# Encoder layer on one core: a feed forward's first weights loaded and split ahead of the last operands, and six pairs of the samples' features instead of four in the filling stream

## The chip, the cores and the metric

The kernel runs on one core of a Trainium2 chip. The metric is the device time of one execution in microseconds, the median of several runs. The core has a matrix engine (TensorE, PE; its weight loads are listed apart as PEld), a vector engine (VectorE, DVE), an activation engine (ScalarE, ACT), a general engine (GpSimd, POOL) and a queue that issues all of this kernel's transfers (SyncE, SP). Each of them works through its own list of instructions in a fixed order and waits at an instruction until what that instruction needs is there.

## What is computed

One layer of an encoder in float32: a gated linear recurrence and a sliding-window attention side by side, a cross-attention into 256 memory tokens, and a SwiGLU feed forward, each followed by a layer norm. It is applied to 1024 prompt tokens and to 8 sample sequences of 16 tokens, so 1152 rows of 1024 columns. The change lies in the feed forward:

```python
def swiglu(x, w_in, w_out):
    g, u = jnp.split(x @ w_in, 2, axis=-1)
    return (jax.nn.silu(g) * u) @ w_out

# post_blocks, last line
x = layer_norm(ALPHA * x + swiglu(x, w_ffn_in, w_ffn_out), ln_g[2], ln_b[2])
```

D_MODEL is 1024, and D_FF is 2816, that is 22 blocks of 128 features, worked in 11 pairs.

## The kernel before

The 1152 rows are nine tiles of 128: eight of the prompt and one (SAMPLE) that holds all the samples. A product in full precision is made of three matmuls: an operand is split into a rounded part ("hi", fp32r, made by a copy on ACT) and a remainder ("lo", made by a subtraction on DVE), and hi*hi, hi*lo and lo*hi are added up. `split` does this; `parts_of` does it for a tile of weights and puts the parts into w_hi and w_lo, of which there are four each.

**The feed forward's first half.** The eight prompt tiles are taken as a 2 x 2 block matrix (two halves of the rows by two halves of the 1024 columns), and each pair's weights too (a11, a12, a21, a22, 512 KB each). Strassen's scheme in Winograd's form needs seven products of 24 matmuls instead of eight: with a11, s1 = a21 + a22, s2 = s1 - a11, s4 = a12 - s2, s3 = a11 - a21, a12 and a22, against the operands B11, T1, T2, B22, T3, B21 and T4. POOL makes the sums s and T. `operands(ops, j, rows)` makes one quarter of the columns of all seven operands, from two token tiles: 16 transposes on PE, four copies on ACT into "stage", four subtractions on POOL into "tt", seven hi parts on ACT and seven lo parts on DVE (that of T4 on POOL). `all_operands` runs it for j = 0 to 3. `hidden(ops, i, then)` computes pair i of the features: it loads the four tiles of weights on SP (line 1003), forms the s, and runs the seven products in the order a11, s1, s2, s4, s3, a12, a22. A product's weights are split as it is issued.

**The samples.** Their features use plain float32 matmuls against the weights as loaded, 64 PE instructions in the trace a pair. In pairs 0 to FILL - 1 `filler` does it: it loads each of the four weight tiles a second time, into one of three w_raw tiles (line 971), 16 PE instructions a tile, which is called a chunk here. Each pair takes two of the four banks "a" of PSUM, and ends with three steps of `sample_gated`, one on ACT (line 959) and two on DVE (lines 960 and 961), and a store of the result (hs_scratch, line 962). Since there are four banks, pair i + 2 needs those of pair i, which the three steps read. In the later pairs `sample_pair` does it inside `hidden`, between the first and the second product, from the weights that are there already; in the last pair at the end.

**What sets the order.** The program is written by streams (generators) that an Order object takes in turn, by ranks and by a count of estimated matmul time. all_operands has rank 6 and filler rank 10, so the chunks stand between the operands of j and j + 1. The feed forward waits for both streams (`yield ready`, `yield filled`) and then goes through the eleven pairs. Within this the framework's scheduler may move an instruction a little on its engine. So all engines' lists are fixed when the program is built, SP's list of transfers too: a transfer that waits holds all that stand behind it.

Of the kernel before, what the change touches and what calls it, by code (L numbers as in the profile page):

```python
# [10 lines left out]
F32R = mybir.dt.float32r  # L11
# [7 lines left out]
P = 128  # L19
# [11 lines left out]
TILES = (0, 1, 3, 4, 5, 6, 7, 8)  # L31
SAMPLE = 2
PAIRS = FT // 2
FILL = 4
PARTS = ((0, 2), (2, 4), (4, 6), (6, 8), (8, 11))


# [65 lines left out]
def trunk(ctx, tc, I, O):  # L103
    nc = tc.nc
# [10 lines left out]
    wp = left.enter_context(tc.tile_pool(name="wp", bufs=1))  # L115
# [4 lines left out]
    N_SLOT, N_TA, N_RAW, N_W = 16, 8, 3, 4  # L120

    def bank(name):
        return pp[name][0].tile([P, 512], F32, name=name, tag=(pp[name] + (name,))[2], bufs=pp[name][1])
# [10 lines left out]
    def split(src, hi, lo, scale=None):  # L134
        if scale is None:
            S.copy(hi, src)  # L136
            V.tensor_tensor(lo, src, hi.bitcast(F32), op=ALU.subtract)  # L137
        else:
            S.activation(hi, src, AF.Copy, scale=scale)
            V.scalar_tensor_tensor(lo, src, scale, hi.bitcast(F32), op0=ALU.mult, op1=ALU.subtract)  # L140

    def raw_tile():
        return wp.tile([P, 1024], F32, name="w_raw", bufs=N_RAW)
# [8 lines left out]
    def mm3(out, a, b, start, stop, **kw):  # L152
        T.matmul(out, a[0], b[0], start=start, stop=False, **kw)
        T.matmul(out, a[0], b[1], start=False, stop=False, **kw)
        T.matmul(out, a[1], b[0], start=False, stop=stop, **kw)

    def cut(pair, *idx):
        return pair[0][idx], pair[1][idx]
# [3 lines left out]
    def cols(t, n=1):  # L162
        return slice(t * P, (t + n) * P)
# [17 lines left out]
    def transposes(src4, n=4):  # L181
        ps = bank("b")
        for j in range(n):
            T.transpose(ps[:, cols(j)], src4[:, cols(j)], ident)
        return ps
# [498 lines left out]
    def big(name, dt=F32):  # L684
        return p2.tile([P, 1024], dt, name=name, tag="big", bufs=10)
# [236 lines left out]
    def operands(ops, j, rows):  # L922

        b = {}
        for q in range(2):
            st = big("stage").rearrange("p (e k c) -> p e k c", e=2, k=4)
            for e in range(2):
                ps = transposes(rows[e][:, q * 512:q * 512 + 512])
                S.copy(st[:, e], ps.rearrange("p (k c) -> p k c", k=4))
                b[f"B{q + 1}{e + 1}"] = st[:, e]  # L930
        for n in range(4):
            if n % 2 == 0:
                tt = big("tt").rearrange("p (a k c) -> p a k c", a=2, k=4)
            b[f"T{n + 1}"] = tt[:, n % 2]
        for o, x, y in (("T1", "B12", "B11"), ("T2", "B22", "T1"), ("T3", "B22", "B12"), ("T4", "B21", "T2")):
            G.tensor_tensor(b[o], b[x], b[y], op=ALU.subtract)
        for o in OPS:
            hi, lo = (x[:, :, cols(j)] for x in ops[o])
            S.copy(hi, b[o])
            (G if o == "T4" else V).tensor_tensor(lo, b[o], hi.bitcast(F32), op=ALU.subtract)  # L940

    def all_operands(ops, rows, ready):
        got = list(rows)

        def load(j):
            got.insert(j, big("x2_row"))
            nc.sync.dma_start(out=got[j], in_=x2_dram[TILES[j]])

        for j in (0, 1, 2, 3, 4):
            load(j)  # L950
        yield 3500.0
        for j in range(4):
            operands(ops, j, (got[j], got[j + 4]))
            yield 6000.0
        order.set(ready, 1000.0)
# [8 lines left out]
    def filler(filled):  # L964

        for i in range(FILL):
            ps = [bank("a")[:, :256] for _ in range(2)]
# [14 lines left out]
    def sample_pair(i, ws):  # L982

        ps = bank("b")
        for e in range(2):
            for z in range(2):
                for kt in range(KT):
                    T.matmul(ps[:, cols(e * 2 + z)], ws[e][kt // 4][:, cols(z * 4 + kt % 4)], xs[:, kt],
                             start=kt == 0, stop=kt == KT - 1)
        g = ps.rearrange("p (e z t) -> p z e t", e=2, z=2)  # L990
        h = hs.rearrange("p (e t) -> p e t", e=2)
        sample_gated(i, h, [g[:, 0], g[:, 1]])

    def parts_of(src, hi, lo):
        split(src, hi, lo)
        return hi, lo

    def hidden(ops, i, then):

        def wt(name, j=None):  # L1000
            t = big(name)
            if j is not None:
                nc.sync.dma_start(out=t, in_=I["w_f1"][i, j])
            return t

        th = [raw_tile() for _ in range(2)]
        m1 = raw_tile()
        m1 = [m1[:, :512], m1[:, 512:]]
        a11, a21, a22, a12 = wt("a11", 0), wt("a21", 2), wt("a22", 3), wt("a12", 1)
        s1, s2, s4 = wt("s1"), wt("s2"), wt("s4")  # L1010
        G.tensor_tensor(s1, a21, a22, op=ALU.add)
        G.tensor_tensor(s2, s1, a11, op=ALU.subtract)
        G.tensor_tensor(s4, a12, s2, op=ALU.subtract)
        m0 = [big("m0") for _ in range(2)]

        t1, t2, t4 = m0[0][:, 512:], m0[1][:, 512:], m1[0]
        X, Z, W = [], [], []

        def product(bk, which, w, op, start):
            pair = parts_of(w, *(wp.tile([P, 1024], F32R, name=x, bufs=N_W) for x in ("w_hi", "w_lo")))  # L1020
            for z in range(2):
                if start:
                    bk.append(bank(which))
                for kt in range(4):
                    mm3(bk[z], cut(pair, ALL, cols(z * 4 + kt)), cut(ops[op], ALL, kt),
                        start and kt == 0, kt == 3, skip_group_check=not start)
                yield z

        def gated(t, gate, up):
            S.activation(t, gate, AF.Tanh, scale=0.5)  # L1030
            V.scalar_tensor_tensor(t, t, 1.0, gate, op0=ALU.add, op1=ALU.mult)
            V.scalar_tensor_tensor(t, t, 0.5, up, op0=ALU.mult, op1=ALU.mult)

        def store(o, src):

            nc.sync.dma_start(out=h_dram[:, OPS.index(o), :, i].rearrange("q p b c -> p q b c"),
                              in_=src.rearrange("p (q b c) -> p q b c", b=2, c=P))

        a, b = slice(0, 512), slice(512, 1024)
        for z in product(X, "a", a11, "B11", True):  # L1040
            S.copy(m0[z][:, a], X[z])
            yield
        last = i == PAIRS - 1
        if FILL <= i and not last:
            sample_pair(i, ((a11, a12), (a21, a22)))
        s3 = wt("s3") if last else a21
        G.tensor_tensor(s3, a11, a21, op=ALU.subtract)
        for z in product(Z, "b", s1, "T1", True):
            S.copy(m1[z], Z[z])
            yield  # L1050
        for z in product(X, "a", s2, "T2", False):
            S.copy(m0[z][:, b], X[z])
            yield
        for z in product(Z, "b", s4, "B22", False):
            V.tensor_tensor(m0[z][:, b], m0[z][:, b], Z[z], op=ALU.add)
            yield
        then()
        gated(th[0][:, b], m0[0][:, b], m0[1][:, b])
        for z in product(X, "a", s3, "T3", False):
            V.tensor_tensor(m1[z], m1[z], X[z], op=ALU.add)  # L1060
            yield
        gated(th[1][:, b], m1[0], m1[1])
        for z in product(W, "b", a12, "B21", True):
            V.tensor_tensor(m0[z][:, a], m0[z][:, a], W[z], op=ALU.add)
            yield
        gated(th[0][:, a], m0[0][:, a], m0[1][:, a])
        G.tensor_tensor(t1, th[0][:, b], th[0][:, a], op=ALU.subtract)
        G.tensor_tensor(t2, th[1][:, b], t1, op=ALU.subtract)
        G.tensor_tensor(th[0][:, b], th[1][:, b], th[0][:, b], op=ALU.subtract)
        for o, src in (("B11", th[0][:, a]), ("T1", t1), ("T2", t2), ("B22", th[1][:, b]), ("T3", th[0][:, b])):  # L1070
            store(o, src)
        for z in product(X, "a", a22, "T4", False):
            yield
        if last:
            sample_pair(i, ((a11, a12), (a21, a22)))
        gated(th[1][:, a], X[0], X[1])
        G.tensor_tensor(t4, th[1][:, a], t2, op=ALU.subtract)
        store("B21", th[1][:, a])
        store("T4", t4)
# [387 lines left out]
```

## Time and profile before

| what | value |
|---|---|
| time, median of 3 runs | 1707.23 us (1706.56 to 1713.33) |
| time of the profiled execution | 1704.64 us |
| span of its trace | 1702.9 us |
| samples' stream and operands, the first chunk at 845.6 to the last at 882.6 | 37 us |
| first product of pair 0 to the second product's start | 890.53 to 904.92 |
| eleven hidden pairs to their last matmul of samples | to 1382.2 |
| second half of the feed forward | from 1382.2 |

The times in the trace are microseconds from the span's start. L96 is the matmul's line, L100 the transposes', L136 and L137 the two halves of a split. The trace leaves out numbers in names, so a11, a12, a21 and a22 all read "a" where they are loaded, and s1, s2 and s4 read "s"; the bank "a" of PSUM has the same letter. "both" holds the samples' activations and their features. A bracket at a row's end is the time that the engine sat idle before it, and what ended it.

### The profile page before, as it was taken

Reading aid. Unit: us, or ns where it says so; the run is one execution under the profiler, and the core shown is the slowest. Engines: PE = TensorE matmul, PEld = TensorE weight load, DVE = VectorE, ACT = ScalarE, POOL = GpSimd, SP = SyncE. Lnnn points to the kernel's source line nnn. Section 1 sums busy time; section 2 is a strip of 40 time slices with the busy share of each in tenths; the row PEclk is TensorE's granted clock in tenths of the full one; section 3 lists DMA queues with packets and bytes.
Section 4 is the critical chain, followed back from the end, with each engine's and each line's share of the span. In section 5 each row is a group of like instructions: output and inputs, shape, how many; then the busy total and the mean of one; then the engine's idle time right before and its main releaser. Section 6 shows DMA issues by size and latency. Waiting matters only on the chain.

```text
span 1702.9 us, 24403 instructions
## 1 busy us (share of the span) xinstructions
PE 1620.7 (95%) x9065; PEld 1391.3 (82%) x9065; DVE 1134.6 (67%) x2021; ACT 674.4 (40%) x1365; POOL 495.7 (29%) x381
## 2 busy tenths in 40 slices
PE   8999999999999999999979999999999969988896
PEld 7998999999888987889877888888888857766674
DVE  6786788778488666786687454544444665767576
ACT  4543555446443544325263333323222333434321
POOL 1111111111000000000074443332333454676555
PEclk9999999999999999999998999999999988999998
DMA  7443343334974687556362333122222245333342
GB/s 239 143 160 122 102 148 104 98 118 137 314 274 154 197 278 268 198 171 236 115 205 78 104 115 117 66 74 86 95 92 96 93 164 180 105 118 118 103 146 95
DMA packets 114358, 247.91 MB, mean 146 GB/s; under 512 B 11840, under 2 KB 58048, under 8 KB 114240
## 3 DMA queue, kind: packets, MB, share of 16 engines
q1 hardware_dynamic: 114240, 246.36, 43.8%
q8 instruction: 71, 1.16, 0.3%
q14 instruction: 47, 0.39, 0.1%
HBM read 203.65 MB, written 42.60 MB: 145 GB/s over the span
## 4 chain that ended last, share of the span: by engine, by line
PE 77%; DVE 7%; DMA 6%; POOL 5%; ACT 2%; issue 2%; SPq 1%; POOLq 0%; ACTq 0%; DVEq 0%
PE a L96 48%; PE b L96 20%; PE x L96 3%; PE b L100 2%; DMA hq<-h_scratch 2%; PE z L96 1%; DVE w L1122 1%; PE s L96 1%; DMA raw<-in_w_f_dram 1%; PE w L96 1%; DVE y L1164 1%; DMA w_raw<-in_w_out_dram 1%; DMA w_raw<-in_w_fm_dram 1%; DMA w_raw<-in_w_f_dram 1%; DVE w_lo L137 1%
## 5 line engine op out<-in xcount | busy, mean ns | idle before, releaser
L137 DVE TENSOR_TENSOR w_lo<-w_raw,w_hi 128x1024 fp32r<-128x1024 f32 (+1 forms) x169 | 204.8, 1214 | 115.0 <-ACT w_hi L136 114.6
L136 ACT CAST w_hi<-w_raw 128x1024 fp32r<-128x1024 f32 (+1 forms) x169 | 174.6, 1034 | 206.1 <-PE a L96 77.4
L96 PE MATMUL a<-w_hi,q_hi 128*128 128x256 f32 (+1 forms) x576 | 197.4, 344 | 0.8 <-ACT kv_sb L270 0.7
L96 PE MATMUL a<-w_lo,q_hi 128*128 128x256 f32 (+1 forms) x576 | 196.9, 342 | 0.0
L96 PE MATMUL a<-w_hi,q_lo 128*128 128x256 f32 (+1 forms) x576 | 194.7, 338 | 0.0
L96 PE MATMUL a<-q_hi,w_hi 128*128 128x384 f32 x528 | 186.8, 354 | 7.3 <-ACT q_hi L136 4.3
L96 PE MATMUL a<-q_hi,w_lo 128*128 128x384 f32 x528 | 179.9, 341 | 0.0
L96 PE MATMUL a<-q_lo,w_hi 128*128 128x384 f32 x528 | 179.5, 340 | 0.0
L96 PE MATMUL x<-w,hh 128*128 128x512 f32 x344 | 115.0, 417 | 39.5 <-DVE y L1164 23.6
L137 DVE TENSOR_TENSOR w_lo<-a,w_hi 128x1024 fp32r<-128x1024 f32 x43 | 75.0, 1743 | 76.9 <-ACT w_hi L136 76.9
L96 PEld LDWEIGHTS a<-w_hi,q_hi 128*128 128x128 f32 x576 | 108.4, 188 | 15.6 <-ACT kv_sb L270 1.1
L96 PEld LDWEIGHTS a<-w_lo,q_hi 128*128 128x128 f32 x576 | 108.6, 189 | 13.3 <-issue 1.2
L96 PEld LDWEIGHTS a<-w_hi,q_lo 128*128 128x128 f32 x576 | 108.5, 188 | 12.7 <-issue 0.2
L96 PEld LDWEIGHTS x<-w,hh 128*128 128x128 f32 x344 | 66.6, 198 | 62.8 <-ACT hh L1152 15.7
L96 PEld LDWEIGHTS a<-q_hi,w_hi 128*128 128x128 f32 x528 | 100.5, 190 | 12.2 <-ACT q_hi L136 4.6
L699 POOL TENSOR_TENSOR rs<-rs,mhalf 128x1 f32<-128x1 f32 x18 | 17.2, 958 | 301.0 <-DVE rs L698 301.0
L96 PE MATMUL a<-T_h,w_hi 128*128 128x512 f32 x264 | 104.7, 396 | 0.0
L96 PE MATMUL a<-T_l,w_hi 128*128 128x512 f32 x264 | 104.7, 396 | 0.0
L96 PE MATMUL a<-T_h,w_lo 128*128 128x512 f32 x264 | 104.6, 396 | 0.0
L96 PEld LDWEIGHTS a<-q_lo,w_hi 128*128 128x128 f32 x528 | 100.7, 191 | 1.6 <-issue 0.9
L96 PEld LDWEIGHTS a<-q_hi,w_lo 128*128 128x128 f32 x528 | 100.2, 190 | 1.0 <-DVE w_lo L137 0.7
L1152 ACT CAST hh<-hq 128x512 fp32r<-128x512 f32 (+2 forms) x75 | 46.3, 619 | 133.2 <-DMA hq<-h_scratch 117.3
(308 smaller groups left out, 3930.4 us busy)
## 6 DMA issues: line engine op xcount, KB each, us to landing
a<-in_w_f_dram SPq DMA_DIRECT2D x44, 512.0 KB, 5.2
w_raw<-in_w_fm_dram SPq DMA_DIRECT2D x41, 512.0 KB, 3.9
h_scratch<-w_raw SPq DMA_DIRECT2D x55, 256.0 KB, 2.2
hq<-h_scratch SPq DMA_DIRECT2D x54, 256.0 KB, 2.7
w_raw<-in_w_tm_dram SPq DMA_DIRECT2D x24, 512.0 KB, 3.5
w_raw<-in_w_out_dram SPq DMA_DIRECT2D x24, 512.0 KB, 5.7
w_raw<-in_w_mq_dram SPq DMA_DIRECT2D x24, 512.0 KB, 4.2
w_raw<-in_w_mo_dram SPq DMA_DIRECT2D x24, 512.0 KB, 4.4
```

Of the source, the lines that this page charges most:

```text
L96: return self.eng.matmul(out, lhsT, rhs, **kw)
L100: return self.eng.transpose(out, in_, identity)
L136: S.copy(hi, src)
L137: V.tensor_tensor(lo, src, hi.bitcast(F32), op=ALU.subtract)
L699: G.tensor_tensor(rs, rs, mhalf[:, 0:1], op=ALU.pow)
L1122: (G if name in ("A21", "A22") else V).tensor_tensor(lo, src, hi.bitcast(F32), op=ALU.subtract)
L1152: S.copy(hi, q)
L1164: V.scalar_tensor_tensor(y[b, e][:, hs], y[b, e][:, hs], 1.0 if key in y else ALPHA, ps, op0=ALU.mult, op1=ALU.add)
```

## The change

`FILL` goes from 4 to 6, so `filler` computes the samples' features of pairs 4 and 5 too, with eight more loads and chunks, and `sample_pair` no longer runs in these two pairs. And pair 0's four weight tiles are loaded, and a11 split, by a new function `begin(0)`, which all_operands calls ahead of the operands of j = 3; `hidden` takes them from there, and calls begin itself in the other pairs.

```diff
--- before.py
+++ after.py
@@ -31,7 +31,7 @@
 TILES = (0, 1, 3, 4, 5, 6, 7, 8)
 SAMPLE = 2
 PAIRS = FT // 2
-FILL = 4
+FILL = 6
 PARTS = ((0, 2), (2, 4), (4, 6), (6, 8), (8, 11))
 
 
@@ -950,6 +950,8 @@
             load(j)
         yield 3500.0
         for j in range(4):
+            if j == 3:
+                begun.append(begin(0))
             operands(ops, j, (got[j], got[j + 4]))
             yield 6000.0
         order.set(ready, 1000.0)
@@ -995,19 +997,28 @@
         split(src, hi, lo)
         return hi, lo
 
+    begun = []
+
+    def begin(i):
+
+        def wt(name, j):
+            t = big(name)
+            nc.sync.dma_start(out=t, in_=I["w_f1"][i, j])
+            return t
+
+        a11, a21, a22, a12 = wt("a11", 0), wt("a21", 2), wt("a22", 3), wt("a12", 1)
+        return a11, a21, a22, a12, parts_of(a11, *both_parts())
+
+    def both_parts():
+        return tuple(wp.tile([P, 1024], F32R, name=x, bufs=N_W) for x in ("w_hi", "w_lo"))
+
     def hidden(ops, i, then):
 
-        def wt(name, j=None):
-            t = big(name)
-            if j is not None:
-                nc.sync.dma_start(out=t, in_=I["w_f1"][i, j])
-            return t
-
+        a11, a21, a22, a12, first = begun.pop() if begun else begin(i)
         th = [raw_tile() for _ in range(2)]
         m1 = raw_tile()
         m1 = [m1[:, :512], m1[:, 512:]]
-        a11, a21, a22, a12 = wt("a11", 0), wt("a21", 2), wt("a22", 3), wt("a12", 1)
-        s1, s2, s4 = wt("s1"), wt("s2"), wt("s4")
+        s1, s2, s4 = big("s1"), big("s2"), big("s4")
         G.tensor_tensor(s1, a21, a22, op=ALU.add)
         G.tensor_tensor(s2, s1, a11, op=ALU.subtract)
         G.tensor_tensor(s4, a12, s2, op=ALU.subtract)
@@ -1017,7 +1028,7 @@
         X, Z, W = [], [], []
 
         def product(bk, which, w, op, start):
-            pair = parts_of(w, *(wp.tile([P, 1024], F32R, name=x, bufs=N_W) for x in ("w_hi", "w_lo")))
+            pair = first if w is a11 else parts_of(w, *both_parts())
             for z in range(2):
                 if start:
                     bk.append(bank(which))
@@ -1043,7 +1054,7 @@
         last = i == PAIRS - 1
         if FILL <= i and not last:
             sample_pair(i, ((a11, a12), (a21, a22)))
-        s3 = wt("s3") if last else a21
+        s3 = big("s3") if last else a21
         G.tensor_tensor(s3, a11, a21, op=ALU.subtract)
         for z in product(Z, "b", s1, "T1", True):
             S.copy(m1[z], Z[z])
```

In the rows that follow, the lists of the built programs are shown, with the numbers of the tiles and the semaphores that each row waits for. The lines of the new program are counted anew (973 was 971, 964 was 962, 1006 was 1003, 962 and 963 were 960 and 961). First SP, from the load of the samples' pair 3, second chunk, on; before:

```order
L971 DMA w_raw_9793<-in_w_f1_dram 128x1024 [waits DMAHW4_49,DMAHW0_49,PE_49]
L971 DMA w_raw_9803<-in_w_f1_dram 128x1024 [waits DMAHW1_49,PE_49]
L971 DMA w_raw_9859<-in_w_f1_dram 128x1024 [waits DMAHW2_49,PE_49]
L962 DMA hs_scratch<-both_84 128x256 [waits DVE_49]
L1003 DMA a11_9876<-in_w_f1_dram 128x1024 [waits Activation_49,Pool_49]
L1003 DMA a21_9878<-in_w_f1_dram 128x1024 [waits Activation_49,Pool_49]
L1003 DMA a22_9880<-in_w_f1_dram 128x1024 [waits Pool_49]
L962 DMA hs_scratch<-both_84 128x256 [waits DMAHW3_49,DVE_49]
L1003 DMA a12_9882<-in_w_f1_dram 128x1024 [waits DMAHW4_49]
L1003 DMA a11_10133<-in_w_f1_dram 128x1024 [waits DMAHW5_49,Activation_49,Pool_49]
```

and with the change, at the same place:

```order
L973 DMA w_raw_9793<-in_w_f1_dram 128x1024 [waits DMAHW4_49,DMAHW0_49,PE_49]
L1006 DMA a11_9813<-in_w_f1_dram 128x1024 [waits Pool_49]
L973 DMA w_raw_9803<-in_w_f1_dram 128x1024 [waits DMAHW1_49,PE_49]
L1006 DMA a21_9815<-in_w_f1_dram 128x1024
L964 DMA hs_scratch<-both_84 128x256 [waits DVE_49]
L1006 DMA a22_9817<-in_w_f1_dram 128x1024
L1006 DMA a12_9819<-in_w_f1_dram 128x1024 [waits DMAHW2_49]
L973 DMA w_raw_9871<-in_w_f1_dram 128x1024 [waits DMAHW3_49,PE_49]
L973 DMA w_raw_9887<-in_w_f1_dram 128x1024 [waits DMAHW4_49,PE_49]
L973 DMA w_raw_9897<-in_w_f1_dram 128x1024 [waits DMAHW6_49,DMAHW5_49,PE_49]
```

The load of a11 now stands between the loads of pair 3's second and third chunk, those of a21, a22 and a12 around the store of pair 2, and the last chunk of pair 3 and the first two of pair 4 follow. Before, the store of pair 3 (the second hs_scratch) was followed by a12 and by the next pair's weights. Further on in SP's new list stands:

```order
L973 DMA w_raw_9907<-in_w_f1_dram 128x1024 [waits DMAHW3_49,PE_49]
L973 DMA w_raw_9917<-in_w_f1_dram 128x1024 [waits DMAHW7_49,DMAHW4_49,PE_49]
L964 DMA hs_scratch<-both_84 128x256 [waits DMAHW0_49,DVE_49]
L973 DMA w_raw_9933<-in_w_f1_dram 128x1024 [waits DMAHW5_49,DMAHW1_49,PE_49]
L973 DMA w_raw_9943<-in_w_f1_dram 128x1024 [waits DMAHW6_49,DMAHW2_49,PE_49]
L973 DMA w_raw_9953<-in_w_f1_dram 128x1024 [waits DMAHW7_49,PE_49]
L964 DMA hs_scratch<-both_84 128x256 [waits DVE_49]
L973 DMA w_raw_9963<-in_w_f1_dram 128x1024 [waits DMAHW1_49,PE_49]
L964 DMA hs_scratch<-both_84 128x256 [waits DVE_49]
L1006 DMA a11_10222<-in_w_f1_dram 128x1024 [waits Activation_49,Pool_49]
```

Here w_raw_9917 is the last chunk of pair 4, and w_raw_9933, 9943, 9953 and 9963 are those of pair 5. The first three of these stand behind the store of pair 3, the fourth behind the store of pair 4, and the next hidden pair's a11 behind that of pair 5. The second place is DVE, from the last lo part of the operands (B21 of j = 3) on; a_9781 and a_9782 are pair 3's banks. Before:

```order
L940 TENSOR_TENSOR B21_l_9492<-stage_9826,B21_h_9491 128x4x128 [waits Activation_49]
L960 SCALAR_TENSOR_TENSOR both_84<-both_84,a_9781 128x256 [waits Activation_49]
L961 SCALAR_TENSOR_TENSOR both_84<-both_84,a_9782 128x256 [waits DVE_49,PE_49]
L137 TENSOR_TENSOR w_lo_9893<-a11_9876,w_hi_9892 128x1024 [waits DMAHW0_49,Activation_49]
L137 TENSOR_TENSOR w_lo_9926<-s1_9884,w_hi_9925 128x1024 [waits Activation_49]
L137 TENSOR_TENSOR w_lo_9958<-s2_9885,w_hi_9957 128x1024 [waits Activation_49]
L137 TENSOR_TENSOR w_lo_9988<-s4_9886,w_hi_9987 128x1024 [waits Activation_49]
L137 TENSOR_TENSOR w_lo_10021<-a21_9878,w_hi_10020 128x1024 [waits PE_49,Activation_49]
```

and with the change, where a_9885 and a_9886 are pair 4's banks, a_9931 and a_9932 pair 5's:

```order
L940 TENSOR_TENSOR B21_l_9492<-stage_9838,B21_h_9491 128x4x128 [waits Activation_49]
L137 TENSOR_TENSOR w_lo_10018<-s1_9980,w_hi_10017 128x1024 [waits Activation_49]
L137 TENSOR_TENSOR w_lo_10050<-s2_9981,w_hi_10049 128x1024 [waits Activation_49]
L962 SCALAR_TENSOR_TENSOR both_84<-both_84,a_9781 128x256 [waits Activation_49]
L137 TENSOR_TENSOR w_lo_10080<-s4_9982,w_hi_10079 128x1024 [waits Activation_49]
L963 SCALAR_TENSOR_TENSOR both_84<-both_84,a_9782 128x256 [waits DVE_49,PE_49]
L962 SCALAR_TENSOR_TENSOR both_84<-both_84,a_9885 128x256 [waits Activation_49]
L963 SCALAR_TENSOR_TENSOR both_84<-both_84,a_9886 128x256 [waits DVE_49,PE_49]
L962 SCALAR_TENSOR_TENSOR both_84<-both_84,a_9931 128x256 [waits Activation_49]
L963 SCALAR_TENSOR_TENSOR both_84<-both_84,a_9932 128x256 [waits DVE_49,PE_49]
```

The two steps of pair 3 have moved from ahead of the four splits to either side of the split of s4, that of a11 has gone ahead of the operands of j = 3 (it stands six rows above), and the steps of pairs 4 and 5 follow. POOL's list makes s1, s2 and s3, then T4's remainder, then s4, where it made T4's remainder first. The third place is PE, from the last chunk of the samples' stream on; before:

```order
L96 MATMUL a_9781<-both_84,w_raw_9859 128x128 [waits DMAHW6_49]
L96 MATMUL a_9781<-both_84,w_raw_9859 128x128 x3
L96 MATMUL a_9782<-both_84,w_raw_9859 128x128 x4
L96 MATMUL a_9896<-B11_h_9481,w_hi_9892 128x512 [waits DVE_49,Activation_49]
L96 MATMUL a_9896<-B11_l_9482,w_hi_9892 128x512 [waits DVE_49]
L96 MATMUL a_9910<-B11_h_9481,w_hi_9892 128x512 [waits PE_49]
L96 MATMUL a_9896<-B11_h_9481,w_lo_9893 128x512 [waits DVE_49]
```

and with the change, from pair 4's last chunk on:

```order
L96 MATMUL a_9885<-both_84,w_raw_9917 128x128 [waits DMAHW7_49]
L96 MATMUL a_9885<-both_84,w_raw_9917 128x128 x3
L96 MATMUL a_9886<-both_84,w_raw_9917 128x128 x4
L96 MATMUL b_10021<-T1_h_9483,w_hi_10017 128x512 [waits PE_49,Activation_49]
L96 MATMUL a_9931<-both_84,w_raw_9933 128x128 [waits DMAHW1_49,DVE_49]
L96 MATMUL a_9931<-both_84,w_raw_9933 128x128 x3
L96 MATMUL a_9932<-both_84,w_raw_9933 128x128 [waits DVE_49]
L96 MATMUL a_9932<-both_84,w_raw_9933 128x128 x3
L96 MATMUL a_9931<-both_84,w_raw_9943 128x128 [waits DMAHW2_49]
L96 MATMUL a_9931<-both_84,w_raw_9943 128x128 x3
L96 MATMUL a_9932<-both_84,w_raw_9943 128x128 x4
```

Between pair 4 and the product of a11 PE now has pair 5's chunks (two are shown in these rows, the other two and then the 24 matmuls of B11 follow), and one matmul of T1 has come ahead of them. a_9931 and a_9932, pair 5's banks, wait for DVE, which reads pair 3's features from the same two banks.

## The prediction

> **What bounds the kernel now.** First the page: TensorE (PE) is busy for nearly the whole span, and most of the chain that ended last is PE's own.
>
> ```profile
> span 1702.9 us, 24403 instructions
> PE 1620.7 (95%) x9065; PEld 1391.3 (82%) x9065; DVE 1134.6 (67%) x2021; ACT 674.4 (40%) x1365; POOL 495.7 (29%) x381
> PE 77%; DVE 7%; DMA 6%; POOL 5%; ACT 2%; issue 2%; SPq 1%; POOLq 0%; ACTq 0%; DVEq 0%
> ```
>
> So an edit is worth what it does to PE's idle time and to PE's work. The second view cuts the feed forward into stretches: the samples' stream with the operands of the eight token tiles, the wait at the first product of the first hidden pair, and then the hidden pairs.
>
> ```profile
> 840.00:884.60 44.60, 42.80 (x345) 40.50 (x344) 34.69 (x41) 21.86 (x42) 26.08 (x19) 1.00 0.59 193
> 884.60:904.90 20.30, 9.02 (x24) 6.71 (x25) 20.16 (x12) 7.87 (x12) 17.42 (x8) 0.66 0.60 187
> 904.90:1062.30 157.40, 157.40 (x673) 126.58 (x672) 83.44 (x85) 52.25 (x68) 64.53 (x31) 1.00 0.27 93
> 1062.30:1341.40 279.10, 279.10 (x1394) 232.81 (x1394) 133.10 (x138) 81.31 (x108) 96.66 (x49) 1.00 0.25 87
> ```
>
> The columns are the length, then the busy time of PE, PEld, DVE, ACT and POOL with the number of instructions, then the granted clock, the DMA share and GB/s. From 904.9 on PE is busy for every microsecond of a stretch. Before that lie 20.3 us in which PE is busy for 9.0. There DVE is the full one (20.16 of 20.30) with POOL next. The timeline of PE shows that stretch from within:
>
> ```profile
> 882.61 1.95 PE L96 MATMUL a<-both,w_raw 128*128 128x128 f32 x16
> 890.53 0.80 PE L96 MATMUL a<-B_h,w_hi 128*128 128x512 f32 x1 [5.98 <-ACT w_hi L136]
> 897.53 0.80 PE L96 MATMUL a<-B_h,w_lo 128*128 128x512 f32 x1 [5.35 <-DVE w_lo L137]
> 898.13 0.63 PE L96 MATMUL a<-B_h,w_hi 128*128 128x512 f32 x1
> 898.55 0.63 PE L96 MATMUL a<-B_l,w_hi 128*128 128x512 f32 x1
> 902.39 0.58 PE L96 MATMUL a<-B_h,w_lo 128*128 128x512 f32 x1
> 903.28 0.40 PE L96 MATMUL a<-B_h,w_lo 128*128 128x512 f32 x1
> 903.51 0.39 PE L96 MATMUL a<-B_h,w_hi 128*128 128x512 f32 x1
> 904.92 0.40 PE L96 MATMUL b<-T_h,w_hi 128*128 128x512 f32 x1
> ```
>
> The last chunk of the samples' stream starts at 882.61. Then PE waits 5.98 us for the rounded half (w_hi) of a11 and 5.35 us for its remainder (w_lo). From 897.53 the matmuls start 0.42 us apart, from 902.8 0.23 us apart: for 4.9 us after the idle time PE runs at half speed. The second product starts at 904.92. **That start is the mark of this prediction**: behind it PE has no gap until the hidden pairs end, so whatever moves it moves the end, and whatever is taken from PE's work behind it is gained whole.
>
> **What the change removes.** Pairs 4 and 5 no longer have their samples' matmuls between their first and second product. In pair 4 these stand here:
>
> ```profile
> 1062.35 1.05 PE L96 MATMUL b<-both,a 128*128 128x128 f32 x8
> 1069.42 0.48 PE L96 MATMUL b<-T_h,w_hi 128*128 128x512 f32 x1
> ```
>
> That is 7.07 us of PE without a gap, and 0.07 us for the slower first matmul behind it: 7.1 us a pair, **14.2 us for two**. They are sure, since the stretch 904.90 to 1062.30 (pairs 0 to 3, which have no such matmuls) already runs without idle time.
>
> **What it adds and moves.** Eight chunks of the samples' stream, 16 instructions each on PE, are added ahead of the first product, and the idle time of 11.3 us is what should hide them. A chunk is 1.87 us of PE:
>
> ```profile
> 872.82 3.74 PE L96 MATMUL a<-both,w_raw 128*128 128x128 f32 x32
> 877.13 3.89 PE L96 MATMUL a<-both,w_raw 128*128 128x128 f32 x32 [0.58 <-DMA w_raw<-in_w_f_dram]
> DMA to landing us min/median/max: 3.3/4.2/6.0
> ```
>
> (The last row is from the view of the loading line, L971: 512 KB each, from issue to landing.) Whether the idle time can be filled is decided by the order of the rows shown with the change. Pair 5's four loads stand on SP behind the store of pair 3's features (hs_scratch), which waits for DVE's last step of pair 3; pair 5's banks wait for the same step; and DVE now has that step behind w_lo<-s4, the last split of the first four weights. PE has all B11 matmuls behind pair 5's last chunk. So the chain is: operands of j = 3 on POOL, s1, s2, s3, s4, w_hi, w_lo, DVE's step of pair 3, store, load, four chunks, first product. In the kernel before the first product waited only for a11.
>
> 1. **DVE's step of pair 3.** In the rows of before:
>
> ```profile
> 882.65 1.28 POOL L936 TENSOR_TENSOR tt<-stage 128x512 f32<-128x512 f32 x1 [1.52 <-ACT stage L929]
> 889.34 1.55 POOL L940 TENSOR_TENSOR T_l<-tt,T_h 128x512 fp32r<-128x512 f32 x1 [0.73 <-ACT T_h L939]
> 890.86 2.79 POOL L1011 TENSOR_TENSOR s<-a,a 128x1024 f32<-128x1024 f32 x1
> 893.72 2.68 POOL L1012 TENSOR_TENSOR s<-s,a 128x1024 f32<-128x1024 f32 x1
> 899.88 3.12 POOL L1013 TENSOR_TENSOR s<-a,s 128x1024 f32<-128x1024 f32 x1 [0.18 <-DMA a<-in_w_f_dram]
> 889.09 0.68 DVE L940 TENSOR_TENSOR B_l<-stage,B_h 128x512 fp32r<-128x512 f32 x1
> 891.36 2.83 DVE L940 TENSOR_TENSOR B_l<-stage,B_h 128x512 fp32r<-128x512 f32 x1
> 894.63 0.42 DVE L961 SCALAR_TENSOR_TENSOR both<-both,a 128x256 f32<-128x256 f32 x1
> 894.96 2.52 DVE L137 TENSOR_TENSOR w_lo<-a,w_hi 128x1024 fp32r<-128x1024 f32 x1
> 897.40 7.95 DVE L137 TENSOR_TENSOR w_lo<-s,w_hi 128x1024 fp32r<-128x1024 f32 x3
> 881.50 2.05 ACT L929 COPY stage<-b 128x512 f32<-128x512 f32 x4 [1.72 <-PE b L100]
> 889.45 1.03 ACT L136 CAST w_hi<-a 128x1024 fp32r<-128x1024 f32 x1
> ```
>
> The last split, w_lo<-s4, ends at 897.40 + 7.95 = 905.35, and the step of pair 3 (L961) was over at 895.05, ahead of it. The change keeps the same work on POOL and DVE up to that split. Three things shift it. The transposes of j = 3 stand behind a chunk whose load now follows a11's: I take 0.6 us, from nothing to 1.8 (the landing's 6.0 less its median 4.2). The 0.73 us that POOL waited ahead of T_l and the 0.18 us for a12 go: -0.9. The split of a11 comes ahead of the first of POOL's steps of j = 3, and these two engines take turns here: the same B_l takes 0.68 us alone and 2.83 us beside s1, ending 0.54 us after s1's end (893.65). So POOL's step waits for the split: up to +1.1, which is w_lo's own time (897.48 less the 896.40 at which s2 ended), and not below nothing. I take it whole. Sum +0.8: the split ends at 906.15, the step 0.45 later, **at 906.6** (bounds 905.0 and 908.5).
>
> The other moved pieces cost nothing here. ACT's w_hi<-a11 (1.03 us in the old place) now precedes ACT's copies of j = 3, ahead of which ACT waited 1.72 us; a11's load follows the one of 873.47, and with a landing of 4.2 to 6.0 it is there by 880. T4's remainder moves on POOL from ahead of s1 to behind s3, and only the seventh product reads it. The loads of a21, a22 and a12 come earlier than their first reader, s1, wants them.
>
> [...]
>
> 2. **Store and load.** SP's rows give what passes between them:
>
> ```profile
> 858.43 10.57 SPq L971 DMA_DIRECT2D w_raw<-in_w_f_dram  x6
> 873.47 3.44 SPq L971 DMA_DIRECT2D w_raw<-in_w_f_dram  x3
> 895.07 0.33 SPq L962 DMA_DIRECT2D hs_scratch<-both  x1
> 895.45 9.05 SPq L1003 DMA_DIRECT2D a<-in_w_f_dram  x5
> ```
>
> The store was issued 0.02 us after L961's end, and the load behind it 0.38 us later. With the median landing of 4.2 and 0.05 to PE that is 4.65 us (3.75 to 6.45 by the landing's ends): the first chunk of pair 5 starts at 911.25.
>
> 3. **Four chunks.** Pair 4's chunks are loaded from about 884 on, and with a22 and a12 ahead of them and 1.75 us a load (10.57 us for six) the last lands by about 900; with one early matmul of T1 PE is idle from about 902 on, more than the 5.35 us that in this trace made it run at half speed for 4.9 us. Four chunks are 4 x 1.87 = 7.5 us; the slow 4.9 us do only half their work, +2.45: 9.9 us (7.5 if PE stayed warm). The fourth load needs the slot of the first chunk, so it is issued some 3.7 us in and lands 3.3 to 6.0 later, at 7.0 to 9.7, where PE comes to it at 8.0: hidden at the median, at most +1.7.
>
> [...]
>
> 4. **First product.** 24 matmuls of 0.234 us are 5.6; one matmul of the second product ran early, so 5.4. The second product then starts at 911.25 + 9.9 + 5.4 = **926.55**, against 904.92: 21.6 us later.
>
> **Sum:** 21.6 - 14.2 = +7.4 us, on the profiled execution's 1704.64 us: 1712.0. The three runs shown have a median of 1707.23, which is 2.6 above the profiled one, so on that scale **1714.6 us**, 0.43% over before. The early split of a11 is right and ready long before its product, but its product is no longer next in line. What hides the rest: the next pair's weights, whose loads now follow pair 5's store, are wanted 39 us after the first product's start and land some 10 us after it.
>
> **The rivals.** *The filler fills the gap* (chance 0.06). If pair 5's loads were not held, eleven loads from 883.6 at 1.75 us each would land by 903, the first product would end at 908.3 and the time would be 3.4 - 14.2 = -10.8 us: 1696.4. For it speaks only that DVE could come to pair 3's step early; against it that step's place in DVE's order, behind s4, which four steps of 1024 columns on POOL must precede: the mark would have to start before 919.1, so the step be over by 899.1, while s4 alone began at 899.88.
>
> *The refill is dearer* (chance 0.34), the rival on the slow side: the loads behind the store. If the first lands at the view's 6.0 instead of 4.2, or a11's load holds the chunk of j = 3 by 1.8 instead of 0.6, the mark moves by 1.8 or 1.2 more: +9.2 or +8.6, 1716.4 or 1715.8. It decides from 1.1 us above the forecast, which is where 0.5% (8.5 us) lies; that is also about what a measurement of this kernel can tell from no change.
>
> *The samples' matmuls were not on the path* (0.01): pairs 4 and 5 would show idle time in their place, and the time would be +21.6, 1728.8. The gapless pairs 0 to 3 speak against it.
>
> **How the numbers follow.** Forecast, between no change and +8.5 us, 0.59, with 1714.6. All bounds together low (905.0, 3.75, 7.5) give +2.5, or 1709.7; all high (908.5, 6.45, 9.9 + 1.7) give +13, or 1720. The range 1708.0 to 1719.0 leaves out the first rival and the high corner and has 1.5 us for the runs' own spread. Faster by over 0.5%: 0.06; within 0.5%: 0.59; slower by over 0.5%: 0.35.
>
> **What would show it.** Right: PE idle for some 9 us ahead of pair 5's first chunk, released by a DMA of w_raw; the store of pair 3 issued at 906 to 907 right behind L963 of DVE, itself behind w_lo<-s; pair 5's first chunk at half speed; the second product at 925 to 928 and pairs 4 and 5 at 39.4 us each without a gap. Wrong: pair 5's loads issued before 900, or the mark before 919 (then it is faster), or idle time in pairs 1 to 5.

## The result and the profile after

| | before | after |
|---|---|---|
| median | 1708.98 us (17 runs, 1706.56 to 1713.33) | 1713.57 us (17 runs, 1709.22 to 1718.76) |
| ratio, 95% interval | | 1.0027 (1.0018 to 1.0037) |
| profiled execution | 1704.64 us | 1713.75 us |

The ratio is 4.6 us on 1709, with 3.1 and 6.3 as its ends: a little slower, by less than 0.5%. The first lines of the page and its line on the chain that ended last:

```profile
span 1711.9 us, 24425 instructions
PE 1623.5 (95%) x9065; PEld 1396.2 (82%) x9065; DVE 1127.0 (66%) x2021; ACT 674.7 (39%) x1365; POOL 506.7 (30%) x381
PE 75%; DVE 7%; DMA 6%; POOL 5%; ACT 3%; issue 2%; SPq 0%; POOLq 0%; ACTq 0%; DVEq 0%
```

They hardly differ from before: the change lies in one place of some 40 us. The stretches of the feed forward (length, busy time of PE, PEld, DVE, ACT and POOL, granted clock, DMA share, GB/s) show it, cut behind the operands' last transposes, at the mark, after six pairs and after four more:

```profile
842.50:887.10 44.60, 41.03 (x329) 38.63 (x328) 35.29 (x41) 21.43 (x41) 24.71 (x18) 1.00 0.62 204
887.10:929.07 41.97, 26.48 (x170) 24.85 (x170) 20.22 (x16) 9.17 (x16) 19.80 (x9) 0.80 0.51 175
929.07:1165.17 236.10, 236.10 (x1010) 189.83 (x1009) 120.38 (x126) 78.39 (x102) 106.61 (x47) 1.00 0.27 96
1165.17:1351.20 186.03, 186.03 (x929) 155.16 (x929) 88.78 (x92) 54.24 (x72) 65.70 (x33) 1.00 0.25 87
```

Six pairs now take 236.10 / 6 = 39.35 us each without idle time, where four did, so pairs 4 and 5 have lost their samples' matmuls as forecast. But ahead of them lie 42.0 us in which PE is busy for 26.5. The timeline of PE within:

```profile
886.11 0.60 PE L100 MATMUL b<-ident,rows 128*128 128x128 f32 x4
893.24 6.98 PE L96 MATMUL a<-both,w_raw 128*128 128x128 f32 x42 [6.54 <-DMA w_raw<-in_w_f_dram]
904.44 0.48 PE L96 MATMUL b<-T_h,w_hi 128*128 128x512 f32 x1
914.27 9.34 PE L96 MATMUL a<-both,w_raw 128*128 128x128 f32 x64 [9.35 <-DMA w_raw<-in_w_f_dram]
923.36 0.48 PE L96 MATMUL a<-B_h,w_hi 128*128 128x512 f32 x1
929.07 0.39 PE L96 MATMUL b<-T_l,w_hi 128*128 128x512 f32 x1
```

PE waits twice for a transfer of samples' weights: 6.54 us for the last chunk of pair 3, and 9.35 us for the first of pair 5. The second wait is the forecast one. Who ends the two is read from POOL, ACT, DVE and SP:

```profile
901.53 2.25 POOL L940 TENSOR_TENSOR T_l<-tt,T_h 128x512 fp32r<-128x512 f32 x1
903.74 3.32 POOL L1024 TENSOR_TENSOR s<-a,s 128x1024 f32<-128x1024 f32 x1
899.79 0.38 ACT L961 ACTIVATE both<-a 128x256 f32<-128x256 f32 x1
907.10 1.04 ACT L136 CAST w_hi<-s 128x1024 fp32r<-128x1024 f32 x1 [6.93 <-POOL s L1024]
904.78 0.41 DVE L962 SCALAR_TENSOR_TENSOR both<-both,a 128x256 f32<-128x256 f32 x1
908.17 1.23 DVE L137 TENSOR_TENSOR w_lo<-s,w_hi 128x1024 fp32r<-128x1024 f32 x1 [2.98 <-ACT w_hi L136]
909.32 0.41 DVE L963 SCALAR_TENSOR_TENSOR both<-both,a 128x256 f32<-128x256 f32 x1
886.03 0.33 SPq L964 DMA_DIRECT2D hs_scratch<-both  x1
886.40 0.93 SPq L1006 DMA_DIRECT2D a<-in_w_f_dram  x2
887.43 12.04 SPq L973 DMA_DIRECT2D w_raw<-in_w_f_dram  x5
909.76 0.33 SPq L964 DMA_DIRECT2D hs_scratch<-both  x1
910.18 1.34 SPq L973 DMA_DIRECT2D w_raw<-in_w_f_dram  x3
918.05 0.33 SPq L973 DMA_DIRECT2D w_raw<-in_w_f_dram  x1
```

Of pair 3's two steps on DVE the first (L962) is over at 905.19. The second needs nothing more, but stands behind w_lo<-s4. DVE idles for 2.98 us until ACT has rounded s4, splits it, and only then does the second step, which ends at 909.73. The store goes out 0.03 us later, the loads 0.42 us after the store, and PE starts at 914.27. SP had issued nothing since 899.47 (887.43 + 12.04).

The first wait has a store ahead of it too, that of pair 2 (886.03). In the new list the load of pair 3's last chunk stands behind this store and behind a22 and a12, and goes out at 887.43 as the first of the five. Before, it was the last of the three loads from 873.47 on (a row in the prediction) and went out by 876.91, well ahead of that store. This is SP's row in before:

```profile
883.16 0.33 SPq L962 DMA_DIRECT2D hs_scratch<-both  x1
```

### The profile page after: what moved, and what is told of

Its sections match the earlier page's. It is cut to its first block, busy times and chain, and to the rows that moved or that the text cites. A ratio compares the mean times of both kernels' runs of the same rounds, so it can differ in the third digit from the quotient of the medians.

```text
span 1711.9 us, 24425 instructions
## 1 busy us (share of the span) xinstructions
PE 1623.5 (95%) x9065; PEld 1396.2 (82%) x9065; DVE 1127.0 (66%) x2021; ACT 674.7 (39%) x1365; POOL 506.7 (30%) x381
## 4 chain that ended last, share of the span: by engine, by line
PE 75%; DVE 7%; DMA 6%; POOL 5%; ACT 3%; issue 2%; SPq 0%; POOLq 0%; ACTq 0%; DVEq 0%
PE a L96 45%; PE b L96 19%; PE x L96 4%; PE b L100 2%; PE z L96 2%; DMA hq<-h_scratch 2%; PE w L96 1%; PE s L96 1%; DVE w_lo L137 1%; DMA raw<-in_w_f_dram 1%; DMA w_raw<-in_w_f_dram 1%; DMA w_raw<-in_w_out_dram 1%; ACT w_hi L136 1%; DVE w L1133 1%; POOL hl L1164 1%
```

## The experiments

Each kernel was timed against the kernel before on the same chip. The traces are compared by one number: from the stream's first chunk to the mark (the second product's start; where that product itself has gaps, the third's start less 5.62 us, one product). Two more profiles of before and one of after give its scatter.

> The kernel before, profiled a second time: if the profiled execution that the sum started from was a short one in the stage that the change touches, the second product starts some 2 us later than its 59.3 us after the stream's first chunk; if not, at 59.3 again. The time 1704 to 1712.

> The kernel before, profiled a third time, for the spread of the same number: 59 to 62 us. The time 1704 to 1712.

> The changed kernel unaltered, with the others on one chip: 1711 to 1712 where before has 1707, by the ratio 1.0027 measured; in its trace the second product 78 to 82 us after the stream's first chunk if the store's chain is what sets it.

The three profiles of before have 59.3, 60.1 and 59.5 us (mean 59.6), the two of after 80.9 and 82.1. So the stage of before was no short one, and the supposition of 2 us falls. The second mark of after lies 0.1 us beyond the 78 to 82 expected. The first idle time of before repeats to a hundredth of a microsecond, those of after to 0.3 us. These are PE's row in the second profile of before, and its two rows in the second profile of after:

```profile
892.83 0.79 PE L96 MATMUL a<-B_h,w_hi 128*128 128x512 f32 x1 [5.97 <-ACT w_hi L136]
```

```profile
894.99 8.79 PE L96 MATMUL a<-both,w_raw 128*128 128x128 f32 x64 [6.73 <-DMA w_raw<-in_w_f_dram]
915.77 10.25 PE L96 MATMUL a<-both,w_raw 128*128 128x128 f32 x64 [9.06 <-DMA w_raw<-in_w_f_dram]
```

The kernel after, timed again, was 1713.94 us against 1708.85: 1.0037 (1.0024 to 1.0049), some 6 us over before where 4 to 5 were expected.

All runs in one table. "By the trace" is the time from the stream's first chunk to the first matmul of the feed forward's second half, less the mean of the three profiles of before (536.9 us); it takes in the mark's shift and what the pairs save behind it. The measured difference is the ratio less one, times 1708.

| kernel | mark, us behind the stream's start | by the trace, us | ratio (95%) | measured, us |
|---|---|---|---|---|
| after (two profiles) | 80.9, 82.1 | +6.8, +8.0 | 1.0027 (1.0018 to 1.0037), 1.0037 (1.0024 to 1.0049) | +4.6, +6.3 |
| early weights alone | 56.7 | -2.8 | 0.9968 (0.9957 to 0.9980) | -5.5 |
| six pairs alone | 67.5 | -6.4 | 0.9952 (0.9935 to 0.9969) | -8.2 |
| early weights, five pairs | 64.3 | -2.5 | 0.9972 (0.9962 to 0.9981) | -4.8 |
| after, joint store | 74.2 | +0.3 | 0.9988 (0.9975 to 1.0001) | -2.0 |
| after, joint store, banks b | 73.9 | 0.0 | 0.9994 (0.9982 to 1.0006) | -1.0 |
| after, steps first | 76.1 | +2.0 | 1.0001 (0.9990 to 1.0013) | +0.2 |
| after, steps first, joint store | 70.4 | -3.5 | 0.9975 (0.9964 to 0.9986) | -4.3 |
| six pairs alone, joint store | 64.7 | -9.2 | 0.9954 (0.9937 to 0.9971) | -7.9 |
| the same, store written after pair 5 | 64.5 | -9.4 | 0.9950 (0.9934 to 0.9966) | -8.5 |

The two columns of microseconds agree within 3 us in every row, so this stretch carries the differences to that accuracy. Smaller differences between rows are not settled by the traces.

**Each half of the change by itself.** The early weights with four pairs:

```diff
-FILL = 6
+FILL = 4
```

> The first weights of the feed forward loaded and split early as in the changed kernel, but only four sample pairs in the stream, as before. Theory A (the change's cost is the wait of pair 5's loads for pair 3's store): without pair 5 there is no such wait. The first product is done as soon as the operands of j = 3 are there, about 902, but the second product's weights (w_lo of s1, then) set the mark: it starts some 54 us after the first chunk of the stream, where before has 59.3, so 3 to 6 us faster than before: 1703 to 1706. Theory B (the eight chunks and the cold TensorE alone eat the gain): the same here, as no chunk is added. Theory C (the early load and split of a11 delay the operands of j = 3 and all that follows): no gain or slower than before, 1709 to 1712.

1701.78 us against 1707.05: the 3 to 6 us of theory A, and theory C (the early split delays all behind it) falls. Its mark came later than expected, at 56.7 and not 54. The first product now starts when the operands of j = 3 come, and the wait has moved to the second product, in PE's and DVE's rows:

```profile
901.37 0.79 PE L96 MATMUL b<-T_h,w_lo 128*128 128x512 f32 x1 [4.67 <-DVE w_lo L137]
```

```profile
899.03 2.28 DVE L137 TENSOR_TENSOR w_lo<-s,w_hi 128x1024 fp32r<-128x1024 f32 x1
901.24 0.41 DVE L962 SCALAR_TENSOR_TENSOR both<-both,a 128x256 f32<-128x256 f32 x1
901.57 3.05 DVE L137 TENSOR_TENSOR w_lo<-s,w_hi 128x1024 fp32r<-128x1024 f32 x1
904.54 0.41 DVE L963 SCALAR_TENSOR_TENSOR both<-both,a 128x256 f32<-128x256 f32 x1
```

Here too pair 3's steps stand between the splits, but no load that PE is about to want waits for them.

Six pairs with the weights loaded late, which is the kernel before with one line changed:

```diff
-FILL = 4
+FILL = 6
```

> Six sample pairs in the stream, the weights loaded and split late as before. DVE then has the step of pair 3 ahead of all splits, at about 895, so pair 5's store and loads are issued some 12 us earlier than in the changed kernel. Theory A: the mark starts at about 908.5 in before's times, 3.6 us later than before, against 14.2 us saved: about 10.6 us faster than before, 1698.4. Theory B (the eight chunks keep TensorE waiting on loads wherever they stand): the mark 18 to 22 us later as in the changed kernel, 1713 to 1717. Theory C (early weights are the harm): faster than the changed kernel by what the early split delays on POOL and DVE, 1 to 2 us: about 1712.

1698.71 us against 1707.05. The same eight chunks that cost time in the changed kernel gain 8.2 us here (interval 5.3 to 11.1), so theory B falls, and theory C with its 1712. The expected 10.6 us lie within the interval; that 1698.71 is so near the expected 1698.4 is luck, since before was faster on this chip. DVE has the steps of pair 3 over at 893.91. SP's rows, and PE's:

```profile
893.93 0.33 SPq L962 DMA_DIRECT2D hs_scratch<-both  x1
894.35 0.89 SPq L971 DMA_DIRECT2D w_raw<-in_w_f_dram  x2
897.10 0.33 SPq L962 DMA_DIRECT2D hs_scratch<-both  x1
897.53 5.01 SPq L971 DMA_DIRECT2D w_raw<-in_w_f_dram  x2
```

```profile
898.59 5.44 PE L96 MATMUL a<-both,w_raw 128*128 128x128 f32 x32 [4.18 <-DMA w_raw<-in_w_f_dram]
914.18 0.50 PE L96 MATMUL b<-T_h,w_lo 128*128 128x512 f32 x1 [0.50 <-DVE w_lo L137]
```

The mark came at 67.5 rather than the 62.9 expected (908.5 less 845.64): PE still waits 4.18 us for a load that is issued right behind pair 3's store.

Early weights with five pairs (FILL = 5):

> The changed kernel with five sample pairs in the stream instead of six: pair 4 runs from its own banks, and nothing waits for pair 3's store. Theory A: the mark moves up by about 19 us against the changed kernel, and one pair's 7.1 us comes back into the hidden stage: 12 us faster than the changed kernel, 7.5 faster than before, 1701.5. Theory B: half of the changed kernel's difference from before, about +2.3: 1711.

1702.32 us against 1707.05, ratio 0.9972: 4.8 us faster than before, where 7.5 were expected, which the interval (3.2 to 6.5) leaves out. Pair 4's banks and loads do not wait for pair 3, so one pair less in the stream is worth 9.4 and 11.1 us against the two ratios of after (12 were expected). Not all waiting for pair 3 has gone: in this trace the first product takes pair 3's banks, and PE idles for 0.88 us at 902.61 and for 1.50 us at 907.19 until DVE has done pair 3's two steps.

**The store.** In the changed kernel the features of pairs 3 and 4 get a tile of their own and one store (the lines that make the tile own_hs and let sample_gated leave out its store are not shown):

```diff
...
+            late = i in (3, 4)
+            h = (own_hs[:, (i - 3) * 256:(i - 2) * 256] if late else hs).rearrange("p (e t) -> p e t", e=2)
+            sample_gated(i, h, [x.rearrange("p (e t) -> p e t", e=2) for x in ps], not late)
+            if i == 4:
+                nc.sync.dma_start(out=hs_dram[:, 3:5], in_=own_hs.rearrange("p (n e t) -> p n e t", n=2, e=2))
...
```

> The changed kernel, but the features of pairs 3 and 4 are held in a tile of their own and stored together after pair 4, so that on SP three of pair 5's four loads are ahead of any store that waits for pair 3. Pair 5's chunks still take the banks that pair 3's step on DVE frees. Theory A: the loads are there when the banks come free at about 909.7, so TensorE starts pair 5 some 4.5 us earlier and the time falls by 4.5 us against the changed kernel: 1709. The fourth load then stands behind the joint store and limits the gain. Theory B (chunks and cold TensorE only): no change, 1713.6.

1705.04 us against 1707.05: 6.7 and 8.4 us below the two ratios of after, more than the 4.5 expected, and not the "no change" of theory B. The 9.35 us before pair 5's chunks shrink to 2.31, and what ends them is no longer a transfer but the banks (PE's row):

```profile
906.07 1.16 PE L96 MATMUL a<-both,w_raw 128*128 128x128 f32 x8 [2.31 <-DVE own_hs L962]
```

With pair 5 in the banks "b" besides (`bank("b" if i == 5 else "a")`):

> The changed kernel with the joint store, and pair 5's chunks in the banks b instead of a, so that they wait for no step of pair 3. With the joint store alone TensorE still stood 2.31 us at pair 5's first chunk for DVE's step, and the last chunk came behind a load issued at 909.33, after the joint store. Theory A: the 2.31 us go, but the last chunk's load, landed at 912.84, ends the stage instead: 1 to 2 us faster than the joint store alone, 1703 to 1704 where before has 1707. Rival (the banks cost nothing): 1705.

1708.96 us against 1708.85, ratio 0.9994: no gain over the joint store alone (0.9988), as the rival had it; theory A expected 1 to 2 us, which the intervals cannot tell from none. The wait for the banks went, and the last chunk's load behind the joint store took its place, in PE's rows:

```profile
906.12 5.60 PE L96 MATMUL b<-both,w_raw 128*128 128x128 f32 x48 [0.86 <-DMA w_raw<-in_w_f_dram]
914.35 2.98 PE L96 MATMUL b<-both,w_raw 128*128 128x128 f32 x16 [2.16 <-DMA w_raw<-in_w_f_dram]
```

**The order alone.** The changed kernel with the splits queued behind the samples' steps on ACT and DVE; nothing else is altered in the source (the lines that collect the steps are not shown):

```diff
...
+    def parts_behind(w, step):
+        with tc.issue_after(step[0]), tc.issue_after(step[1]):
+            return parts_of(w, *both_parts())
...
-            pair = first if w is a11 else parts_of(w, *both_parts())
+            held = 0 if i else 3 if w is s1 else 4 if w is s2 or w is s4 else 0
+            pair = first if w is a11 else parts_behind(w, steps[held]) if held else parts_of(w, *both_parts())
...
```

> The changed kernel with one thing altered, the order on ACT and DVE: the split of s1 is issued behind the steps of the samples' pair 3, and those of s2 and s4 behind the steps of pair 4; loads, splits, chunks and banks are the same. Theory A (pair 3's step behind w_lo<-s4 is what holds the store, and with it pair 5's loads): the step of pair 3 ends at about 900 instead of 909.7, the loads go out then, and the second product starts some 9 to 10 us earlier, 70 to 73 us after the stream's first chunk instead of 81 to 82: 9 us faster than the changed kernel, 1703 to 1706 where before has 1708. Theory B (eight more chunks and a cold TensorE cost it wherever the step stands): no change, 1712 to 1714.

1710.22 us against 1709.36, ratio 1.0001: 4.4 and 6.1 us below the two ratios of after, about half of the 9 us that theory A expected, and not the "no change" of theory B. DVE's, SP's and PE's rows:

```profile
901.16 0.42 DVE L963 SCALAR_TENSOR_TENSOR both<-both,a 128x256 f32<-128x256 f32 x1
901.50 1.44 DVE L137 TENSOR_TENSOR w_lo<-s,w_hi 128x1024 fp32r<-128x1024 f32 x1
909.60 0.42 DVE L963 SCALAR_TENSOR_TENSOR both<-both,a 128x256 f32<-128x256 f32 x1 [0.87 <-PE a L96]
```

```profile
901.61 0.33 SPq L964 DMA_DIRECT2D hs_scratch<-both  x1
902.04 7.88 SPq L974 DMA_DIRECT2D w_raw<-in_w_f_dram  x4
910.04 0.35 SPq L964 DMA_DIRECT2D hs_scratch<-both  x1
911.43 0.33 SPq L974 DMA_DIRECT2D w_raw<-in_w_f_dram  x1
```

```profile
905.93 7.25 PE L96 MATMUL a<-both,w_raw 128*128 128x128 f32 x48 [4.23 <-DMA w_raw<-in_w_f_dram]
914.48 2.05 PE L96 MATMUL a<-both,w_raw 128*128 128x128 f32 x16 [1.30 <-DMA w_raw<-in_w_f_dram]
```

The step of pair 3 ends 53.9 us behind the stream's start (901.58 less 847.64), 7.6 earlier than the 61.6 of after. The mark gains 4.8. The rest is given back on SP, whose list has shifted in the built program: the store of pair 3 now also stands ahead of the load of pair 4's last chunk. PE waits 4.23 us for that chunk, and pair 4 ends late (its step at 910.02). Pair 5's last two loads need the tiles of that chunk and of the next one, and go out as PE is through with them, the second at 911.43. So this run alters the order on SP too, and its 4.8 us are not the price of the splits' place alone. With the joint store as well:

> The run before with the joint store of pairs 3 and 4 after pair 4 as well. Theory A: only the last of pair 5's chunks is still behind a store, and that store is issued at about 904: the second product 67 to 70 us after the stream's first chunk, 2 to 3 us faster than the run before: 1700 to 1703 where before has 1708. Theory B: 1712 to 1714.

1705.51 us against 1709.36: 4.3 us faster than before, where 5 to 8 were expected, and the mark at 70.4 is just beyond the 67 to 70. Against the run before it is 4.4 us faster, by the mark 5.7, and theory B falls. So the order of the steps and the place of the stores are two separate holds.

**The better half, with the joint store.** Six pairs without early weights, where PE still waited 4.18 us behind a store:

> Six pairs in the stream with the weights loaded late, as in the kernel that measured 1698.7, and the features of pairs 3 and 4 stored together after pair 4. In the trace without the joint store TensorE stood 4.18 us ahead of a chunk whose load was issued at 894.35, right behind the store of pair 3, and ran 17 chunk matmuls at half speed after it. Theory A (a store that waits on SP holds the loads behind it): that gap and its slow matmuls go, and a22's load comes earlier; the mark is 3 to 6 us earlier: 1693 to 1696 where before has 1707. Theory B (the three tiles for chunks set the pace of the loads anyway): no gain, 1698.7.

> As the run before, with the joint store written after pair 5 instead of pair 4; on SP it then stands behind all of pair 5's loads and ahead of those of a22 and a12. Theory A: the same chunks or 1 us earlier, but a22 behind the store; s1 and its split wait for a22, so the time is within 2 us of the run before. Theory B: no difference from 1698.7.

1699.35 and 1699.61 us against 1708.85. The marks of the traces show some 3 us (64.7 and 64.5 instead of 67.5), but the times do not: the ratios, 0.9954 and 0.9950, do not differ from 0.9952, and their intervals of 3 us either way could not settle so little. The expected 1693 to 1696 were missed, and theory B of both runs (no difference) is not refuted. In the first of the two traces PE no longer waits 4.18 us, but 2.49 us at 903.19, for a chunk whose load stands behind the joint store. These three kernels beat both of the case by some 8 us (before) and 13 us (after), and which of them is best can't be told.

## Why the prediction was right

Forecast were 1714.6 us, 0.43% over before and within 0.5%; measured were 1713.57 and 0.27% (0.37% the second time). The two times in microseconds are so near in part by luck: the difference was 4.6 us and not 7.4, and before itself, in more runs, came out at 1708.98 and not 1707.23. Against the profiled execution the prediction had +7.4 us, and the mark and the saving of the traces give 21.6 - 14.5 = +7.1. Its steps, each counted from the stream's start, which lay at 845.64 in before and 848.16 in after:

- **DVE's step of pair 3** ended at 909.73 - 848.16 = 61.6, forecast 906.6 - 845.64 = 61.0. What lies within it came partly otherwise than reckoned, as the rows below show.
- **Store and load:** 914.27 - 909.73 = 4.54 us, forecast 4.65.
- **Four chunks:** 923.36 - 914.27 = 9.09 us, forecast 9.9. The half-speed part was 17 matmuls that start 0.213 us apart, 3.6 us, not 4.9, and the fourth load came in time. (The 4.9 us read off before are 5.3: its last slow matmul starts at 902.39, and the next 0.42 us later, at 902.81.)
- **First product:** 929.07 - 923.36 = 5.71 us, forecast 5.4.
- **Saving:** from the mark to the second half's first matmul 477.3 us in before and 462.8 in after, 14.5 less; forecast 14.2.

So the mark moved by 80.9 - 59.3 = 21.6 us, as forecast. That the errors of +0.6, -0.1, -0.8 and +0.3 cancel to nothing is luck.

In the first step two terms were wrong. These are DVE's and POOL's rows in after:

```profile
885.92 1.22 DVE L137 TENSOR_TENSOR w_lo<-a,w_hi 128x1024 fp32r<-128x1024 f32 x1
886.59 1.68 POOL L936 TENSOR_TENSOR tt<-stage 128x512 f32<-128x512 f32 x1 [2.59 <-ACT stage L929]
```

The prediction let POOL's first step of j = 3 wait for the split of a11 (+1.1). It hardly did: it started 0.55 us before that split ended, what ended its wait was ACT's copy, and the split can show in it only as the 0.4 us by which the step itself took longer (1.68 us, in before 1.28). ACT's copy waited 1.80 us (until 885.87) for transposes that stand on PE behind a chunk. The delay that this makes, put at 0.6, was 1.4: POOL's step stands 38.4 us behind the stream's start (886.59 less 848.16), where before had 37.0. So 1.4 came in place of 1.7. POOL's own work took longer here and there: its four subtractions 6.7 us in all instead of 6.0, and T4's remainder 2.25 us between s3 and s4, where it had taken 1.55 ahead of s1; s3 was 0.5 us shorter. All in all the split of s4 ended 0.7 us later than forecast.

Why the sum on the traces (+7.1) is above the measured +4.6 and +6.3, as most sums of the table are, stays open. It is not a short stage of before, which three profiles exclude; the interval of the second measurement (4.1 to 8.4) takes in 7.1 and that of the first (3.1 to 6.3) does not. In the other kernels' traces the rest, from the second half's first matmul to the end, is 317.0 to 320.0 us long, against 320.0 to 320.7 in those of before; that goes the right way for them, but in the two of after it is 320.1 and 320.6.

One idle time was not foreseen: 6.54 us ahead of pair 3's last chunk. The prediction had PE idle only "from about 902 on". What makes it is another gate of the kind that the prediction found: the load of that chunk stands on SP behind the store of pair 2 (886.03), and behind a22 and a12. Of the landing's 5.77 us (887.43 to 893.20), 1.6 are above the median of 4.2. In the changed kernel this wait should hardly count, since pair 5 waits in any case for a store that needs w_lo<-s4. The kernel with the steps first has such a wait too (6.26 us at 892.31), and there it lies ahead of all that follows. No run with early weights takes this gate away, so its price is not shown.

The reason behind the forecast holds, too. The rival that the refill is dearer did not decide: the first load landed in 3.95 us (910.18 to 914.13), below the median of 4.2. And that six pairs fill the gap was true only without the early weights: six pairs alone gain 8.2 us, early weights alone 5.5, and both together lose 4.6 to 6.3. With early weights the splits of s1, s2 and s4 stand in DVE's list ahead of the step on which pair 5's loads wait; why the scheduler ordered them so is not shown. What this wait costs is read from the kernels that shorten it: 6.7 to 8.4 us by the joint store, 4.4 to 6.1 by the order, 8.9 to 10.6 by both. The gains of the two halves are no sum to be expected, since both draw on the same 11.3 us of PE's idle time in before. And the wait is not all: with the steps first and the joint store, six pairs with early weights gain 4.3 us, with late weights and the joint store 7.9 (marks 70.4 and 64.7). Where the 5.7 us between these two marks come from was not separated.

## What to carry to other kernels

In these traces a store on the queue that also prefetches is a gate: the loads behind it went out only when its data was ready (in after at 910.18, behind a store held until 909.76). So when work is added to a prefetched stream, look for the store that stands ahead of its loads, and for what stands ahead of the instruction that the store waits for. Two edits that each start something earlier can cost more than both gain, if one of them puts its work ahead of what the other waits for; try them one at a time.

## What was unexpected in the hardware

After idle times of nearly equal length PE ran at half speed in one place and not in another. In the run with the steps first and the joint store:

```profile
882.63 3.78 PE L96 MATMUL a<-both,w_raw 128*128 128x128 f32 x16 [2.73 <-DMA w_raw<-in_w_f_dram]
893.74 7.44 PE L96 MATMUL a<-both,w_raw 128*128 128x128 f32 x64 [2.64 <-DMA w_raw<-in_w_f_dram]
```

After 2.73 us a chunk of 16 took 3.78 us (its matmuls start 0.213 us apart); after 2.64 us 64 matmuls took 7.44 (0.112 us apart). In the run with the banks b, shown above, the last 16 took 2.98 us after an idle time of 2.16, the later ones 0.213 us apart. In the records of the granted clock it is 0.50 in before from 889.12 to 902.78 (13.65 us), and in after from 890.69 to 897.52 (6.83 us) and from 907.76 to 918.00 (10.24 us; the 0.80 over 41.97 us shown above). The shortest stretch at 0.50 lasts 3.41 us in both traces (from 168.91 in before, from 1518.74 in after), and the three lengths are four, two and three times that. Each of the three begins within an idle time of PE: 4.6, 4.0 and 2.8 us behind its start (884.55 in before, 886.70 and 904.92 in after). Why nearly equal idle times fell on either side is not shown.

The wait of a store is seen on the queue: in after SP issues nothing from 899.47 to 909.76, and the loads go out 0.42 us behind the store that waited.
